# A hybrid decoder layer on one core: the first projection block starts on unscaled k tiles, which are rescaled later

## The chip, the core and the metric

The kernel runs on one core of one Trainium2 chip. The core has a matrix engine (PE, with its weight loads PEld), a vector engine (DVE), an activation engine (ACT), a general engine (POOL) and a queue engine (SP) that issues most of the loads. Each engine works through its own list of instructions in order and waits on semaphores of the others. The metric is the time of one execution in microseconds (us).

## The reference, cut to what matters

One decoder layer: RMSNorm of x (512 tokens by 2048), one wide input projection, two token mixers (an mLSTM and a gated DeltaNet branch), an output projection, merge gates, a residual and a final RMSNorm, all in float32. What matters here is the front:

```python
y = x * rsqrt(mean(x * x, -1) + 1e-6) * norm_w      # u, 512 x 2048
proj = u @ w_in                                      # 2048 x 20528
```

Each token of u carries a factor, rsqrt(...), that is known only when the whole row of x has been read and squared; norm_w is a factor per channel. A product with unscaled channels can be scaled by the token's factor afterwards, since that factor is common to all channels of the token.

## The kernel before

x is cut into 4 chunks of 128 tokens, the 2048 channels into 16 k tiles of 128 (`KT`). A float32 product is made of three passes in the type fp32r: high half by high half, low by high, high by low. So every operand is split: ACT casts a copy to the high half (`split_hi`, L140) and DVE subtracts to get the low half (`split_lo`, L143). u is kept with tokens on the free side, as `uh` (high) and `ul` (low), 16 tiles of 128 x 512.

**Start.** SP loads the four chunks of x, two halves each. ACT and DVE square and sum each chunk, POOL takes the power -1/2 (L304), ACT and DVE scale the chunk (`scale_x`, L290 and L292). Only then can PE transpose the four 128 x 128 pieces of a k tile (`make_u`, L313); ACT writes `uh`, DVE `ul` (L314, L315), both with norm_w's column as scale.

**The four front blocks** (`proj_cm`, L257 to L259) are 256 columns each of q and k. A block goes over 8 pairs of k tiles; the weights of one pair are one *part* here: a load into `wr`, a cast into `wh` and a difference into `wl`, in rotating sets of 4 buffers (`NSPL`), prepared up to 3 parts ahead. Parts 0 to 7 are block 1, 8 to 15 block 2, 16 to 23 block 3, 24 to 31 block 4. A part has 24 products in two half steps (one for each 128 columns), and after each half step `tick()` lets small jobs run. In block 1 the same loop also makes the u tiles, two ahead, and the products of the 48 gate columns (`gate_products`, L324, L325), eight k tiles late.

**Jobs beside blocks 2 to 4.** `gates()` turns the gate columns into per-token rows: transposes of the block's sum `gr0` on PE (`pgt`, L401), some 30 short DVE operations that compute softplus, and 20 ticks later twelve transposes (`pri`, `prf`, `prg`, L443 to L445) of their results, the scans, and a last set of transposes (`pc`). `u_sums()` adds tiles of u for the stage that follows (L373 to L384). `lead()` loads that stage's first weights. The seven stage (PE lines L578 to L580) begins when block 4 ends.

**What sets the order.** PE's list is as written. On the other engines a list scheduler sets it by priority and a timeline of its own.

Of the kernel before, what the change touches and what calls it, by code (L numbers as in the profile page):

```python
# [15 lines left out]
P = 128  # L16
# [12 lines left out]
GLAG = 8  # L29
# [29 lines left out]
def hybrid_body(  # L59
# [91 lines left out]
    plan = [("i", (ML_Q, ML_K)[a] + b * NB, k) for a, b in QK for k in range(0, KT, KP)]  # L151
# [10 lines left out]
    limit = [nfront]  # L162

# [11 lines left out]
    def split_next():  # L175
        raw, nk, n = raws[len(parts)]
        with tc.high_priority(offset=2 * PRIO if len(parts) > SAHEAD else 0):
            hi = wp.tile([P, nk, n], F32R, tag="wh", name="wh", bufs=NSPL)
            lo = wp.tile([P, nk, n], F32R, tag="wl", name="wl", bufs=NSPL)
            with ExitStack() as first:  # L180
                if not parts:
                    first.enter_context(behind("V"))
                    first.enter_context(behind("A"))
                elif len(parts) == 1:
                    first.enter_context(tc.issue_after(done["V"]))
                    first.enter_context(tc.issue_after(done["A"]))
                split_hi(hi, raw)
                split_lo(lo, raw, hi)
        parts.append((hi, lo))

    def prepare(i):
        while len(raws) < min(limit[0], i + RAHEAD + 1):
            load_raw()
        while len(parts) < min(limit[0], i + SAHEAD + 1):
            split_next()
# [50 lines left out]
    def proj_cm(col0, before=None):  # L246
        ps = [psj.tile([P, S], F32, tag="pj", name="pj") for _ in range(2)]
        for kt0 in range(0, KT, KP):
            hi, lo = next_w("i", col0, kt0)
            if before is not None:  # L250
                for k in range(KP):
                    before(kt0 + k)
            for j in range(2):
                for k in range(KP):
                    kt = kt0 + k
                    wsl = slice(j * P, (j + 1) * P)
                    T.matmul(ps[j], hi[:, k, wsl], uh[:, kt, :], start=(kt == 0), stop=False)  # L257
                    T.matmul(ps[j], hi[:, k, wsl], ul[:, kt, :], start=False, stop=False)  # L258
                    T.matmul(ps[j], lo[:, k, wsl], uh[:, kt, :], start=False, stop=(kt == KT - 1))  # L259
                tick()  # L260
        return ps
# [4 lines left out]
    xts = []  # L266
    for c in range(NC):
        xt = p0.tile([P, D], F32, tag=f"x{c}", name=f"xt{c}")
        for i in range(2):
            nc.sync.dma_start(xt[:, i * HD:(i + 1) * HD], x[c * P:(c + 1) * P, i * HD:(i + 1) * HD])  # L270
        xts.append(xt)
    for _ in range(2):
        load_raw()
# [3 lines left out]
    wgh, wgl = wgp[:, :, 0:48], wgp[:, :, 64:112]  # L277
    G.memset(wgp[:, :, 48:64].bitcast(F32), 0.0)
    taps = []
    ss = p0.tile([P, NC, 2], F32, tag="ss", name="ss")  # L280
    rs = p0.tile([P, NC], F32, tag="rs", name="rs")
    mhalf = cp.tile([P, NC], F32, tag="mhalf", name="mhalf")
    G.memset(mhalf, -0.5)
    half = cp.tile([P, 2, NC], F32, tag="half", name="half")
    G.memset(half, 0.5)
    sq, done = {}, {}

    def scale_x(c):
        with tc.issue_after(sq["V"]):
            newest["V"] = V.tensor_scalar(out=xts[c][:, 0:HD], in0=xts[c][:, 0:HD], scalar1=rs[:, c:c + 1], scalar2=None,  # L290
                                        op0=ALU.mult).ins
        newest["A"] = A.mul(xts[c][:, HD:D], xts[c][:, HD:D], rs[:, c:c + 1]).ins  # L292

    for c in range(NC):
        xt = xts[c]
        jk = p0.tile([P, HD], F32, tag="jk", name="jk", bufs=2)
        A.activation(jk, xt[:, 0:HD], AF.Square, accum_out=ss[:, c, 0:1])
        jv = p0.tile([P, HD], F32, tag="jv", name="jv", bufs=2)
        sq["V"] = V.scalar_tensor_tensor(out=jv, in0=xt[:, HD:D], scalar=1.0, in1=xt[:, HD:D], op0=ALU.mult, op1=ALU.mult,
                                         accum_out=ss[:, c, 1:2]).ins  # L300
        V.tensor_tensor(out=rs[:, c:c + 1], in0=ss[:, c, 0:1], in1=ss[:, c, 1:2], op=ALU.add)
        V.tensor_scalar(out=rs[:, c:c + 1], in0=rs[:, c:c + 1], scalar1=1.0 / D, scalar2=EPS,
                        op0=ALU.mult, op1=ALU.add)
        G.tensor_tensor(out=rs[:, c:c + 1], in0=rs[:, c:c + 1], in1=mhalf[:, c:c + 1], op=ALU.pow)  # L304
        if c:
            scale_x(c - 1)
    scale_x(NC - 1)

    def make_u(kt):
        pool, tg = ((psw, "wk"), (pso, "o"))[kt % 2]  # L310
        pt = pool.tile([P, S], F32, tag=tg, name="put")
        for c in range(NC):
            T.transpose(pt[:, c * P:(c + 1) * P], xts[c][:, kt * P:(kt + 1) * P], ident)  # L313
        done["A"] = A.activation(uh[:, kt, :], pt, AF.Copy, scale=normc[:, kt:kt + 1]).ins  # L314
        done["V"] = V.scalar_tensor_tensor(out=ul[:, kt, :], in0=pt, scalar=normc[:, kt:kt + 1],  # L315
                                           in1=uh[:, kt, :].bitcast(F32), op0=ALU.mult, op1=ALU.subtract).ins

    UA = 2
    for kt in range(UA):
        make_u(kt)  # L320
    pgr = psw.tile([P, S], F32, tag="wk", name="pgr")

    def gate_products(kt):
        T.matmul(pgr[0:112, :], wgp[:, kt, :], uh[:, kt, :], start=(kt == 0), stop=False, skip_group_check=True)  # L324
        T.matmul(pgr[0:48, :], wgh[:, kt, :], ul[:, kt, :], start=False, stop=(kt == KT - 1), skip_group_check=True)  # L325

    def first_block(kt):
        if kt == 1:
            nc.sync.dma_start(wg[:, :, 0:16], w_in[:, ML_I:ML_I + 16].rearrange("(k p) n -> p k n", p=P))
            nc.sync.dma_start(wg[:, :, 16:48], w_in[:, DN_B:DN_B + 32].rearrange("(k p) n -> p k n", p=P))  # L330
        if kt == 3:
            taps.extend(load_params(p0))
        if kt == 6:
            with tc.issue_after(done["A"]):
                split_hi(wgh, wg)
            with tc.issue_after(done["V"]):
                split_lo(wgl, wg, wgh)
        if kt == 12:
            turn_taps(*taps, psw)
        if kt + UA < KT:  # L340
            make_u(kt + UA)
        if kt >= GLAG:
            gate_products(kt - GLAG)

# [7 lines left out]
    ps = proj_cm(ML_Q, before=first_block)  # L352
    for kt in range(KT - GLAG, KT):
        gate_products(kt)
    gr0 = wp.tile([112, S], F32, tag="tg", name="gr0", bufs=3)
    A.copy(gr0, pgr[0:112, :])
    spill(ps, 0, float(P) ** -0.5)
# [429 lines left out]
    start(gates())  # L787
    start(u_sums(), 7)
    start(lead(), 38)
    for a, b in QK[1:]:  # L790
        spill(proj_cm((ML_Q, ML_K)[a] + b * NB), 2 * QKFIRST * a + 2 * b, 1.0 if a else float(P) ** -0.5, (a, b) == QK[-1])
# [977 lines left out]
```

## Time and profile before

| what | value |
|---|---|
| time, median of 3 runs | 2154.34 us (2153.77 to 2154.91) |
| time of the profiled execution | 2153.98 us |
| its span, first to last instruction | 2152.2 us |
| PE busy | 2122.7 us, 99% |
| DVE busy | 1710.5 us, 79% |
| ACT busy | 1041.6 us, 48% |

The span is what the profile shows; some 1.8 us of the profiled execution's time lie around it. Shares are means over the whole span: the first 20 us, in which x is loaded and scaled, are no part of what the mean tells.

### The profile page before, as it was taken

Reading aid. Unit: us, or ns where it says so; the run is one execution under the profiler, and the core shown is the slowest. Engines: PE = TensorE matmul, PEld = TensorE weight load, DVE = VectorE, ACT = ScalarE, POOL = GpSimd, SP = SyncE. Lnnn points to the kernel's source line nnn. Section 1 sums busy time; section 2 is a strip of 40 time slices with the busy share of each in tenths; the row PEclk is TensorE's granted clock in tenths of the full one; section 3 lists DMA queues with packets and bytes.
Section 4 is the critical chain, followed back from the end, with each engine's and each line's share of the span. In section 5 each row is a group of like instructions: output and inputs, shape, how many; then the busy total and the mean of one; then the engine's idle time right before and its main releaser. Section 6 shows DMA issues by size and latency. Waiting matters only on the chain.

```text
span 2152.2 us, 31876 instructions
## 1 busy us (share of the span) xinstructions
PE 2122.7 (99%) x10544; PEld 1760.0 (82%) x10544; DVE 1710.5 (79%) x2973; ACT 1041.6 (48%) x1994; POOL 431.5 (20%) x651
## 2 busy tenths in 40 slices
PE   6999999999999999999999999999999999999998
PEld 5888888888888888888888888888888888887886
DVE  5888888788888778777757887887887878569887
ACT  5444444445444444444445545556455464345345
POOL 0000000000004000000002335234233263233221
PEclk9999999999999999999999999999999999999999
DMA  5456676667678767776767777767786677778895
GB/s 162 117 193 191 211 215 196 220 202 227 203 228 243 243 195 223 237 231 195 254 201 176 186 178 185 166 181 188 178 222 171 167 183 209 198 231 278 242 301 230
DMA packets 447143, 444.20 MB, mean 206 GB/s; under 512 B 197121, under 2 KB 303842, under 8 KB 446850
## 3 DMA queue, kind: packets, MB, share of 16 engines
q1 hardware_dynamic: 377618, 337.22, 54.7%
q0 software_dynamic: 24752, 72.90, 10.9%
q10 hardware_dynamic: 44608, 32.06, 4.7%
q8 instruction: 82, 1.34, 0.3%
q14 instruction: 83, 0.68, 0.1%
HBM read 348.66 MB, written 97.58 MB: 207 GB/s over the span
## 4 chain that ended last, share of the span: by engine, by line
PE 94%; DMA 2%; DVE 2%; SPq 1%; issue 1%; ACT 0%; ACTq 0%; DVEq 0%; POOLq 0%; POOL 0%
PE ps L579 17%; PE ps L578 17%; PE ps L580 17%; PE pj L257 9%; PE pj L259 9%; PE pj L258 9%; PE py L1391 2%; PE py L1393 2%; PE py L1392 2%; PE pk L909 1%; PE pqk L979 1%; PE pnum L1197 1%; PE pw L1071 1%; PE po L1086 1%; DMA wr<-in_w_in_dram 0%
## 5 line engine op out<-in xcount | busy, mean ns | idle before, releaser
L140 ACT CAST wh<-wr 128x512 fp32r<-128x512 f32 (+1 forms) x522 | 373.7, 717 | 442.3 <-PE pj L258 233.7
L143 DVE TENSOR_TENSOR wl<-wr,wh 128x512 fp32r<-128x512 f32 (+1 forms) x522 | 439.2, 842 | 171.5 <-ACT wh L140 167.6
L257 PE MATMUL pj<-uh,wh 128*128 128x512 f32 x896 | 376.4, 420 | 0.0
L259 PE MATMUL pj<-uh,wl 128*128 128x512 f32 x896 | 351.3, 392 | 0.0
L258 PE MATMUL pj<-ul,wh 128*128 128x512 f32 x896 | 350.6, 391 | 0.0
L579 PE MATMUL ps<-wl,uh 128*128 128x512 f32 x752 | 292.6, 389 | 0.0
L578 PE MATMUL ps<-wh,uh 128*128 128x512 f32 x752 | 292.6, 389 | 0.0
L580 PE MATMUL ps<-wh,ul 128*128 128x512 f32 x752 | 292.5, 389 | 0.0
L140 ACT CAST wh<-t 128x1024 fp32r<-128x1024 f32 x120 | 126.3, 1053 | 298.4 <-PE ps L580 189.9
L578 PE MATMUL ps<-wh,suh 128*128 128x512 f32 x624 | 242.9, 389 | 0.1
L579 PE MATMUL ps<-wl,suh 128*128 128x512 f32 x624 | 242.8, 389 | 0.0
L580 PE MATMUL ps<-wh,sul 128*128 128x512 f32 x624 | 242.7, 389 | 0.0
L533 POOL DMA_DIRECT2D t_d<-ts x104 | 56.6, 545 | 922.3 <-DVE ts L520 854.0
L140 ACT CAST wh<-ts 128x512 fp32r<-128x512 f32 x240 | 148.4, 618 | 186.8 <-DVE ts L538 157.6
L143 DVE TENSOR_TENSOR wl<-t,wh 128x1024 fp32r<-128x1024 f32 x120 | 146.9, 1224 | 82.1 <-ACT wh L140 81.6
L259 PEld LDWEIGHTS pj<-uh,wl 128*128 128x128 f32 x896 | 168.4, 188 | 37.3
L257 PEld LDWEIGHTS pj<-uh,wh 128*128 128x128 f32 x896 | 169.3, 189 | 30.1
L258 PEld LDWEIGHTS pj<-ul,wh 128*128 128x128 f32 x896 | 169.5, 189 | 28.3
L143 DVE TENSOR_TENSOR wl<-ts,wh 128x512 fp32r<-128x512 f32 x240 | 164.5, 686 | 32.8 <-ACT wh L140 31.3
L579 PEld LDWEIGHTS ps<-wl,uh 128*128 128x128 f32 x752 | 141.2, 188 | 29.7 <-DVE wl L143 0.4
L578 PEld LDWEIGHTS ps<-wh,uh 128*128 128x128 f32 x752 | 141.1, 188 | 29.4
L580 PEld LDWEIGHTS ps<-wh,ul 128*128 128x128 f32 x752 | 141.1, 188 | 29.1
(334 smaller groups left out, 3763.8 us busy)
## 6 DMA issues: line engine op xcount, KB each, us to landing
wr<-in_w_in_dram SPq DMA_DIRECT2D x744, 256.0 KB, 3.7
wr<-in_w_out_dram SPq DMA_DIRECT2D x138, 256.0 KB, 4.7
t_d<-ts POOLq DMA_DIRECT2D x104, 256.0 KB, 3.7
wr<-t_d SPq DMA_DIRECT2D x104, 256.0 KB, 3.8
xt<-in_x_dram SPq DMA_DIRECT2D x8, 512.0 KB, 7.1
tg_d<-X ACTq DMA_DIRECT2D x16, 256.0 KB, 4.7
tg_d<-to ACTq DMA_DIRECT2D x16, 256.0 KB, 4.4
v<-v_d SPq DMA_DIRECT2D x8, 512.0 KB, 6.1
```

What stands on the lines that cost most here:

```text
L140: newest["A"] = A.copy(hi, src).ins
L143: newest["V"] = V.tensor_tensor(out=lo, in0=src, in1=hi.bitcast(F32), op=ALU.subtract).ins
L257: T.matmul(ps[j], hi[:, k, wsl], uh[:, kt, :], start=(kt == 0), stop=False)
L258: T.matmul(ps[j], hi[:, k, wsl], ul[:, kt, :], start=False, stop=False)
L259: T.matmul(ps[j], lo[:, k, wsl], uh[:, kt, :], start=False, stop=(kt == KT - 1))
L533: queue.dma_start(t2_d[b % 2, i], ts[:, 0, :])
L578: T.matmul(ps[t], ah, hi, start=(g == "A" and i == 0), stop=False, skip_group_check=True)
L579: T.matmul(ps[t], ah, lo, start=False, stop=False, skip_group_check=True)
L580: T.matmul(ps[t], al, hi, start=False, stop=(i == KH - 1), skip_group_check=True)
L1391: T.matmul(ps[c], uh[:, kt, tsl], hi, start=(kt == ks[0]), stop=False)
L1392: T.matmul(ps[c], uh[:, kt, tsl], lo, start=False, stop=False)
L1393: T.matmul(ps[c], ul[:, kt, tsl], hi, start=False, stop=(kt == ks[-1]))
```

## The change

x is loaded by columns (all tokens of 256, 256, 512, 256 and 768 channels), with weight loads in between. The first ten k tiles (`KU`) are transposed without the token's factor and multiplied into PSUM banks of their own (`rawp`, `rawg`), while the squares are taken beside the steps. From step 8 on the factor is known: tiles 10 to 15 are scaled as before and multiplied into new banks. The factors are turned into a row (`turn_row`, four products), which scales the raw sums (DVE) and, pair by pair, the ten raw tiles of u (`rescale`, `rescaled`): two pairs in block 1, the third half in it, the rest behind it. Block 2 takes the pairs 10, 12, 14 first. The order of ACT and DVE in block 1 is written by hand. `gates()` starts four ticks later.

```diff
-GLAG = 8
+KU = 10
+    KS[QK[1]] = list(range(KU, KT, KP)) + list(range(0, KU, KP))
...
+    XC = [0, 256, 512, 1024, 1280, D]
+    for n in range(len(XC) - 1):
+        o = slice(XC[n], XC[n + 1])
+        with behind("S") if n else ExitStack():
+            newest["S"] = nc.sync.dma_start(xt[:, :, o], xv[:, :, o]).ins
+        if n in (0, 1, 3, 4):
+            with behind("S"):
+                load_raw()
...
+    def split_u(kt, pt):
+        hi, lo = uh[:, kt, :], ul[:, kt, :]
+        if kt < 4 or kt >= KU:
+            A.activation(hi, pt, AF.Copy, scale=normc[:, kt:kt + 1])
+            V.scalar_tensor_tensor(out=lo, in0=pt, scalar=normc[:, kt:kt + 1], in1=hi.bitcast(F32), op0=ALU.mult, op1=ALU.subtract)
+        else:
+            f = whole(kt - 4, 1)[:, 0]
+            A.activation(f, pt.rearrange("p (c t) -> p c t", t=P), AF.Copy, scale=normc[:, kt:kt + 1])
+            split_hi(hi.rearrange("p (c t) -> p c t", t=P), f)
+            split_lo(lo.rearrange("p (c t) -> p c t", t=P), f, hi.rearrange("p (c t) -> p c t", t=P))
...
+    def rescale(p):
...
+            V.tensor_tensor(out=f, in0=hi.bitcast(F32), in1=lo.bitcast(F32), op=ALU.add)
+        else:
+            f = uf[p] = whole(KP * p - 4, KP)
+        V.tensor_tensor(out=f, in0=f, in1=rr, op=ALU.mult)
...
+    SPLITS = {1: 1, 3: 2, 5: 3, 7: 4, 9: 5, 11: 6, 12: 7, 13: 8, 14: 9, 15: 10}
+    def hook(n):
+        if n in SPLITS:
+            split_next()
...
+        if n == 7:
+            split_hi(wgh, wg)
+            split_lo(wgl, wg, wgh)
+            square(A, 2, 2)
+            square(V, 2, 3)
+            token_factors()
+        if n == 8:
+            scale_x(KU, KU + 2)
+            gps["diag"] = factor_row()
+        if n in (9, 10):
+            for kt in range(KU // 2 * (n - 9), KU // 2 * (n - 8)):
+                gate_products(kt)
+        if n == 10:
+            turn_row(gps["diag"])
...
+        if n + 2 < KT:
+            split_u(n + 2, turn_x(n + 2))
...
+        if n in (11, 13, 15):
+            rescale((n - 11) // 2)
+        if n in (12, 14):
+            rescaled((n - 12) // 2)
+        if n == 10:
+            V.tensor_tensor(out=gr0, in0=rawg[0:112, :], in1=rrow[0:112, :], op=ALU.mult)
...
+    with tc.manual_schedule(engines={mybir.EngineType.Activation, mybir.EngineType.DVE}):
...
+        gsum = V.tensor_tensor(out=gr0, in0=gr0, in1=gps["p"][0:112, :], op=ALU.add).ins
+    with behind("A"), tc.issue_after(gsum):
+        rescaled(2)
+        rescale(3)
+        rescale(4)
+        rescaled(3)
+        rescaled(4)
...
-    start(gates())
+    start(gates(), 4)
```

**Place one: the first scaled tile.** On PE before, all tiles are transposed after scaling, so the list begins with the transposes of tile 0, one from each chunk of x:

```order
L108 MATMUL pprm_126<-ident_76,nrow_124 128x16
L313 MATMUL put_174<-ident_76,xt0_108 128x128
L313 MATMUL put_174<-ident_76,xt1_111 128x128
L313 MATMUL put_174<-ident_76,xt2_114 128x128
L313 MATMUL put_174<-ident_76,xt3_117 128x128
L313 MATMUL put_181<-ident_76,xt0_108 128x128
```

In the changed kernel PE begins on tile 0 without any factor, and the transposes of tile 10 (`put_342`), the first that need it, stand at the head of step 8, ahead of that step's products:

```order
L444 MATMUL pj_142<-ul_90,wh_268 128x512
L445 MATMUL pj_142<-uh_89,wl_269 128x512
L331 MATMUL put_342<-ident_76,xt_113 128x128 x4
L443 MATMUL pj_141<-uh_89,wh_306 128x512
L444 MATMUL pj_141<-ul_90,wh_306 128x512
L445 MATMUL pj_141<-uh_89,wl_307 128x512
L443 MATMUL pj_141<-uh_89,wh_306 128x512
L444 MATMUL pj_141<-ul_90,wh_306 128x512
```

Ahead of them on DVE, the steps 6 to 8 of the changed kernel: the low halves of raw tiles 8 and 9 (`ul`), the split of part 4 (`wl_307`), of the gate weights (`wgp`), the last squares of x, the factors (`rs`), and the scaling of tiles 10 and 11 (L311):

```order
L143 TENSOR_TENSOR ul_90<-xt_113,uh_89 128x512
L143 TENSOR_TENSOR wl_307<-wr_167,wh_306 128x512
L143 TENSOR_TENSOR wgp_128<-wg_127,wgp_128 128x16x48
L298 SCALAR_TENSOR_TENSOR jk_140,ss_134<-xt_113 128x768
L303 TENSOR_REDUCE rs_135<-ss_134 128x4
L304 TENSOR_SCALAR rs_135<-rs_135 128x4
L143 TENSOR_TENSOR ul_90<-xt_113,uh_89 128x512
L311 TENSOR_SCALAR xt_113<-xt_113,rs_135 128x256 x2
```

What moved: the factors stood ahead of all transposes and now stand behind eight steps of them.

**Place two: the gate numbers on DVE.** Before, the last two of them (L431, L434, in `sml`) stand ahead of the split of part 19 (`wl_743`):

```order
L143 TENSOR_TENSOR wl_713<-wr_692,wh_712 128x512
L429 TENSOR_TENSOR sml_546<-sml_546 128x96
L384 TENSOR_TENSOR sul_95<-X_517,suh_94 128x768
L430 SCALAR_TENSOR_TENSOR sml_546<-sml_546 128x96
L384 TENSOR_TENSOR s4l_516<-X_517,s4h_515 128x256
L431 TENSOR_SCALAR sml_546<-sml_546 128x4x8
L434 SCALAR_TENSOR_TENSOR sml_546<-sml_546 128x4x16
L143 TENSOR_TENSOR wl_743<-wr_710,wh_742 128x512
```

In the changed kernel the corresponding operations L545 to L552 stand behind the split of part 23 (`wl_893`), with u sums (`X`, `sul`, `s4l`) in between:

```order
L143 TENSOR_TENSOR wl_893<-wr_839,wh_892 128x512
L493 TENSOR_TENSOR X_548<-X_548 128x256
L495 TENSOR_TENSOR X_548<-X_548 128x256
L546 TENSOR_SCALAR sml_601<-sml_601 128x96
L494 TENSOR_TENSOR X_548<-X_548 128x256
L545 TENSOR_TENSOR sml_601<-sml_601 128x96
L496 TENSOR_TENSOR X_548<-X_548 128x256
L546 TENSOR_SCALAR sml_601<-sml_601 128x96
```

Four rows further on the last eight of these nineteen rows:

```order
L545 TENSOR_TENSOR sml_601<-sml_601 128x96
L546 TENSOR_SCALAR sml_601<-sml_601 128x96
L545 TENSOR_TENSOR sml_601<-sml_601 128x96
L546 TENSOR_SCALAR sml_601<-sml_601 128x96
L547 TENSOR_TENSOR sml_601<-sml_601 128x96
L548 SCALAR_TENSOR_TENSOR sml_601<-sml_601 128x96
L549 TENSOR_SCALAR sml_601<-sml_601 128x4x8
L552 SCALAR_TENSOR_TENSOR sml_601<-sml_601 128x4x16
```

What moved: part 19's place is taken by part 23. On ACT the casts of parts 19 to 23 (`wh_773`, 796, 818, 841, 892) stand so; the fifth of them takes the buffer that the first has, as there are four:

```order
L140 CAST wh_773<-wr_741 128x512
L473 ACTIVATE qk0_766<-pj_556 128x512
L474 DMA qk_d_73<-qk0_766 128x512
L500 CAST suh_94<-X_548 128x768
L140 CAST wh_796<-wr_771 128x512
L500 CAST s4h_546<-X_548 128x256
L140 CAST wh_818<-wr_794 128x512
L140 CAST wh_841<-wr_816 128x512
L500 CAST suh_94<-X_548 128x768
L500 CAST s4h_546<-X_548 128x256
L140 CAST wh_892<-wr_839 128x512
```

**Place three: PE at the gate transposes.** Before, `pri`, `prf` and `prg` come in the middle of part 18 (`wh_712`):

```order
L257 MATMUL pj_738<-uh_89,wh_712 128x512
L258 MATMUL pj_738<-ul_90,wh_712 128x512
L259 MATMUL pj_738<-uh_89,wl_713 128x512
L443 MATMUL pri_797<-ident_76,sml_546 8x128
L444 MATMUL prf_798<-ident_76,sml_546 8x128
L445 MATMUL prg_799<-ident_76,sml_546 16x128
```

In the changed kernel they come when part 19 (`wh_773`) is through:

```order
L250 MATMUL pj_770<-uh_89,wh_773 128x512
L251 MATMUL pj_770<-ul_90,wh_773 128x512
L252 MATMUL pj_770<-uh_89,wl_774 128x512
L561 MATMUL pri_857<-ident_76,sml_601 8x128
L562 MATMUL prf_858<-ident_76,sml_601 8x128
L563 MATMUL prg_859<-ident_76,sml_601 16x128
```

What moved: three half steps later in the blocks, and behind the last product of the part whose buffer the cast of part 23 takes. The row between, `prf`, reads what L549 writes.

## Rows read from the trace of the kernel before

**Rows 1.** The page: the chain of waits that ended last, by engine.

```profile
PE 94%; DMA 2%; DVE 2%; SPq 1%; issue 1%; ACT 0%; ACTq 0%; DVEq 0%; POOLq 0%; POOL 0%
```

**Rows 2.** Waits of PE in total: line, releaser, us, times, longest.

```profile
PE pprm L108 <- POOL rs L304: 14.5, 1, 14.5
PE put L313 <- DVE xt L290: 2.1, 2, 1.3
...
PE ps L578 <- DVE X L1415: 1.5, 1, 1.5
```

**Rows 3.** The chain in order of time, 0 to 160 us: start, us, what.

```profile
17.95 3.03 PE put L313 x13
...
21.41 0.43 PE pj L258
...
23.54 0.36 PE pj L257
...
25.04 0.87 PE put L313 x8
25.91 0.23 PE pj L257
...
58.72 0.39 PE pgt L401 x4
```

**Rows 4.** Timeline of PE, three points: start, us, operation.

```profile
57.17 0.40 PE L257 MATMUL pj<-uh,wh 128*128 128x512 f32 x1
...
86.20 0.27 PE L443 MATMUL pri<-ident,sml 128*8 128x128 f32 x1
...
125.32 0.39 PE L578 MATMUL ps<-wh,suh 128*128 128x512 f32 x1
```

**Rows 5.** Timeline of ACT, 0 to 62 us: the first work on x, its wait.

```profile
4.62 1.06 ACT L297 ACTIVATE jk<-xt 128x1024 f32<-128x1024 f32 x1 [2.59 <-DMA xt<-in_x_dram]
```

**Rows 6.** Timeline of POOL, 0 to 62 us: the last power.

```profile
16.56 0.55 POOL L304 TENSOR_TENSOR rs<-rs,mhalf 128x1 f32<-128x1 f32 x1 [2.07 <-DVE rs L302]
```

**Rows 7.** Groups of ACT by shape, 0 to 175 us: xcount, busy us, mean ns, idle before.

```profile
L140 ACT CAST wh<-wr 128x512 fp32r<-128x512 f32 x40 | 24.5, 619 | 35.2 <-PE pj L258 31.6 <-DMA wr<-in_w_in_dram 3.0 <-PE pj L259 0.5
L314 ACT ACTIVATE uh<-put,normc 128x512 fp32r<-128x512 f32 x16 | 10.5, 686 | 1.4 <-PE put L313 1.2
...
L297 ACT ACTIVATE jk<-xt 128x1024 f32<-128x1024 f32 x4 | 4.2, 1053 | 5.2 <-DMA xt<-in_x_dram 5.2
...
L140 ACT CAST wgp<-wg 128x768 fp32r<-128x768 f32 x1 | 0.8, 834 | 0.0
```

**Rows 8.** Groups of DVE by shape, 0 to 175 us.

```profile
L143 DVE TENSOR_TENSOR wl<-wr,wh 128x512 fp32r<-128x512 f32 x40 | 27.3, 686 | 16.1 <-ACT wh L140 13.9 <-PE put L313 2.2
L315 DVE SCALAR_TENSOR_TENSOR ul<-put,normc,uh 128x512 fp32r<-128x512 f32 x16 | 11.5, 747 | 0.7 <-ACT uh L314 0.2
...
L373 DVE TENSOR_TENSOR X<-uh,ul 128x1024 f32<-128x1024 f32 x8 | 9.7, 1217 | 0.0
L384 DVE TENSOR_TENSOR sul<-X,suh 128x768 fp32r<-128x768 f32 x8 | 7.6, 953 | 0.5 <-ACT suh L382 0.4
...
L375 DVE TENSOR_TENSOR X<-X 128x256 f32<-128x256 f32 x8 | 3.4, 419 | 0.1
L384 DVE TENSOR_TENSOR s4l<-X,s4h 128x256 fp32r<-128x256 f32 x8 | 3.3, 417 | 0.0
...
L427 DVE TENSOR_TENSOR sml<-sml 128x96 f32<-128x96 f32 x7 | 1.8, 253 | 0.1
L428 DVE TENSOR_SCALAR sml<-sml 128x96 f32<-128x96 f32 x7 | 1.4, 206 | 0.1
```

**Rows 9.** Timeline of DVE, 79 to 81 us: the end of the gate numbers.

```profile
78.12 0.95 DVE L384 TENSOR_TENSOR sul<-X,suh 128x768 fp32r<-128x768 f32 x1
78.99 0.25 DVE L430 SCALAR_TENSOR_TENSOR sml<-sml 128x96 f32<-128x96 f32 x1
...
79.58 0.22 DVE L434 SCALAR_TENSOR_TENSOR sml<-sml 128x64 f32<-128x64 f32 x1
```

More of the change, by code (lines that the diff above doesn't have):

```diff
@@ L162, in hybrid_body @@
     limit = [nfront]
+    ahead = [0]
     def load_raw():
@@ L179, in split_next @@
             lo = wp.tile([P, nk, n], F32R, tag="wl", name="wl", bufs=NSPL)
[L180 to L188, printed above, removed]
+            split_hi(hi, raw)
+            split_lo(lo, raw, hi)
         parts.append((hi, lo))
@@ L193, in prepare @@
             load_raw()
-        while len(parts) < min(limit[0], i + SAHEAD + 1):
+        while len(parts) < min(limit[0], i + ahead[0] + 1):
             split_next()
@@ L283, in hybrid_body @@
-    G.memset(mhalf, -0.5)
+    rrow = p0.tile([P, S], F32, tag="rrow", name="rrow")
     half = cp.tile([P, 2, NC], F32, tag="half", name="half")
     G.memset(half, 0.5)
[L286 to L306, printed above, removed]
@@ new lines, in square, with token_factors @@
+    def square(eng, n, c):
+        w = SQ[n].stop - SQ[n].start
+        xc, to = xt[:, c, SQ[n]], ss[:, c, n:n + 1]
+        if eng is V:
+            V.scalar_tensor_tensor(out=jv[:, 0:w], in0=xc, scalar=1.0, in1=xc, op0=ALU.mult, op1=ALU.mult, accum_out=to)
+        else:
+            A.activation(jk[:, 0:w], xc, AF.Square, accum_out=to)
+    def token_factors():
+        V.reduce_sum(out=rs, in_=ss, axis=mybir.AxisListType.X)
+        V.tensor_scalar(out=rs, in0=rs, scalar1=1.0 / D, scalar2=EPS, op0=ALU.mult, op1=ALU.add)
+        G.tensor_tensor(out=rs, in0=rs, in1=mhalf, op=ALU.pow)
@@ new lines, in scale_x, with factor_row @@
+    def scale_x(a, b):
+        for c in range(NC):
+            xc = xt[:, c, a * P:b * P]
+            if c % 2:
+                V.tensor_scalar(out=xc, in0=xc, scalar1=rs[:, c:c + 1], scalar2=None, op0=ALU.mult)
+            else:
+                A.mul(xc, xc, rs[:, c:c + 1])
+    def factor_row():
+        diag = p0.tile([P, NC, P], F32, tag="diag", name="diag")
+        for c in range(NC):
+            V.tensor_scalar(out=diag[:, c, :], in0=ident, scalar1=rs[:, c:c + 1], scalar2=None, op0=ALU.mult)
+        return diag
@@ L311, in make_u, with turn_row, turn_x @@
+    def turn_row(diag):
+        pr = psw.tile([P, S], F32, tag="wk", name="prow")
+        for c in range(NC):
+            T.matmul(pr[:, c * P:(c + 1) * P], ones, diag[:, c, :], start=True, stop=True)
+        A.copy(rrow, pr)
+    def turn_x(kt):
+        pool, tg = ((psw, "wk"), (pso, "o"))[kt % 2 if kt < KU else 0]
         pt = pool.tile([P, S], F32, tag=tg, name="put")
         for c in range(NC):
-            T.transpose(pt[:, c * P:(c + 1) * P], xts[c][:, kt * P:(kt + 1) * P], ident)
@@ new lines, in hook, with first_block @@
+        if n in (11, 13, 15):
[4 more added lines that the diff above has]
+            V.tensor_tensor(out=gr0, in0=rawg[0:112, :], in1=rrow[0:112, :], op=ALU.mult)
+        if n in (12, 14):
+            V.scalar_tensor_tensor(out=qk0[n // 2 - 6], in0=rawp[n // 2 - 6], scalar=QS, in1=rrow, op0=ALU.mult, op1=ALU.mult)
+    def first_block():
+        ps = rawp
+        for n in range(KT):
+            kt0, j = n - n % KP, n % KP
+            if not j:
+                hi, lo = next_w("i", ML_Q, kt0)
+            hook(n)
+            if n == KU:
+                ps = [pso.tile([P, S], F32, tag="o", name="pj") for _ in range(2)]
+            for k in range(KP):
+                kt = kt0 + k
+                wsl = slice(j * P, (j + 1) * P)
+                T.matmul(ps[j], hi[:, k, wsl], uh[:, kt, :], start=(kt in (0, KU)), stop=False)
+                T.matmul(ps[j], hi[:, k, wsl], ul[:, kt, :], start=False, stop=False)
+                T.matmul(ps[j], lo[:, k, wsl], uh[:, kt, :], start=False, stop=(kt in (KU - 1, KT - 1)))
+            if j and kt0 >= KU:
+                for k in range(KP):
+                    gate_products(kt0 + k)
+            tick()
+        return ps
```

124 lines of the change are left out of this document (74 added, 50 removed).

## The prediction

> **What bounds the kernel now.** I read the chain of waits first: PE holds 94% of it [rows 1]. So I took next what PE waits for. Over the whole span it waits 14.5 us for its first transpose, 2.1 us for scaled chunks of x, and afterwards never longer than 1.5 us at a time [rows 2]. Whatever lets PE begin earlier is therefore gained to the end, and whatever it waits for later is lost to the end, unless the work behind shrinks. The chain in order of time shows the start: from 17.95 PE runs unbroken; 13 transposes take 3.03 us, 0.233 each, the first products 0.43 each, and from about 23.6 on a product takes 0.23 and 8 transposes 0.87, 0.109 each [rows 3]. These are the array's two levels, 1.2 and 2.4 GHz: 5.6 us at the lower one, of which half, 2.8 us, is lost. Three points of PE's timeline are my marks: block 2 begins at 57.17, the gate transposes come at 86.20, the seven stage begins at 125.32 [rows 4]. Behind that last mark the lists of DVE and ACT hold the same operations in the same order in both kernels, and PE's list is as written, so I compare the two kernels there and carry the difference to the end.
>
> **The start: minus 12.9 us.** The first 512 KB of x are worked on at 4.62 [rows 5]. The changed kernel's first piece has as many bytes, is issued one place later (behind norm_w) and lies in runs of 1 KB in place of 4 KB; I take 5.04. Nearest rows bound it: 4.6, if neither matters, and 6.0, if the runs cost a quarter. PE's unbroken stretch so begins 12.9 us earlier (12.0 to 13.3). Into it come three slow transposes that lay ahead of 17.95 before, 0.7 us, the four products of the factor row, for which the nearest row is four transposes, 0.44 us [rows 3], and about 0.6 us of short waits (the second piece of x behind the first two tiles, a low half in step 6).
>
> **Tile 10: plus 4.6 us.** The factors are now made beside the raw steps, and the transposes of tile 10 stand at the head of step 8 and wait for them. PE: 16 slow transposes, 9 slow and 3 fast products from 5.04 put tile 4's transposes at 13.4; six steps of four transposes (0.44) and six products (0.23 each), 1.81 a step, and 0.3 of waiting, end at 24.5. ACT can take up tile 4 at 13.95 and then has no pause. A raw tile costs it an activation (0.686) and a cast that depends on it (0.619) where before it was one activation [rows 7]; operations that don't depend on each other overlap by some 0.08, so 1.26 a tile, six tiles 7.6. Three casts of parts add 1.6, the gate weights 0.75 [rows 7]. Three squares of 768 columns have no row of their own; between 0.62 for 512 columns and 1.05 for 1024 [rows 7], with the sum's readout, I take 0.94 each, 2.8. Together 12.75: ACT is through at 26.7. DVE's last square, which has waited behind the gate weights' low half, ends at 27.2; two tiny operations, POOL's power of 0.55 [rows 6] and the hand-overs put the factors at 28.3, two short scalings on ACT put tile 10 at 29.1. PE has waited 4.6 us. If the array is fast earlier and squares cost what 512 columns do, 3; if x's third piece is late, 6.5.
>
> **The end of block 1: plus 2.4 us.** From tile 12's low half (39.2: ten raw gate products a step, the factor row and its copy lie between) DVE has no pause worth a row. Up to the sum of the gate columns it has five 1024-wide adds and products and two 1024-wide differences of the rescaling, 1.14 each (1.217 less the overlap), 8.0; six part splits at 0.605, 3.6; eight operations of the kind of L315 at 0.66 (four low halves, four on the q columns, which ACT did before), 5.3; two sums of the gate columns and the taps, 1.65 [rows 8]. With 0.9 of waiting for ACT that is 19.4, until 58.6. PE would be there at 56.2. So it loses 2.4: about 1.0 at tile 15, the rest at `pgt`. Bounds: 1 and 4, as the broadcast row and the four-dimensional views of the rescaling have no row of their own; the nearest, L373 [rows 8], is what I used.
>
> **The gate transposes: plus 6.8 us.** This is the wait that decides. Before, the gate numbers were done at 79.8 [rows 9], and PE came for them at 86.20 [rows 4]: 6.4 us to spare. In the changed lists PE comes three half steps later in the blocks, when part 19 is through, and DVE has them behind the split of part 23. That split needs ACT's cast, and the cast needs the buffer of part 19, which PE gives back with the very last product ahead of `pri`. So the order alone makes PE wait for one cast (0.619 [rows 7]), one split (0.686) and nineteen operations: four of 256 columns at 0.42, one of 768 at 0.95, another 256 at 0.42, and thirteen of 96 columns or fewer at 0.2 to 0.25 [rows 8], 6.0 end to end, 5.4 with the overlap of 0.08 that the rows show (0.95 long, the next begins 0.87 later [rows 9]). 5.4 and 1.3 and the hand-overs: 6.8 us, 6.0 to 7.5. And DVE isn't there much earlier: its work from 39.2 to that split is 46.3 us (the 18.5 above, then three 1024-wide rescaled differences and two products, eleven splits, three groups of u sums and a begun fourth, and the first half of the gate operations), so it comes to it at 86 to 87, when part 19 ends at 86.5. Were the buffer free earlier, next to nothing would be gained; where DVE is later, the wait grows by that. PE's `prf` holds up all products behind it.
>
> **The clock behind that wait: plus 2.8 us.** After 1.5 us [rows 2] the products go on at the upper level; after the 14.5 us at the start they begin at the lower one and lose 2.8 [rows 3]. No row lies between, so 0 and 2.8 are the ends. 6.8 us is half of the one and over four times the other; I take 2.8. For the 4.6 us at tile 10, in the middle between both, I take 0 and leave 2.8 to a rival.
>
> **The seven stage.** Its first weights go into buffers that the gate rows hold until the `pc` transposes, which also come three half steps later. From these transposes to the first split of that weight there are about 16 us (load 6, DVE's queue 8, cast and split), the blocks leave 18 with the clock at either level. I cost it at nothing; were that cover gone, at most 2 us.
>
> **Sum.** -12.9 + 0.7 + 0.4 + 0.6 + 4.6 + 2.4 + 6.8 + 2.8 = +5.4 us at the mark of 125.32, and from there to the end. The profiled execution took 2153.98, which is 0.36 below the median of the runs: 2159.4 us. Block 2 would begin at about 51.7 (5.5 earlier than before), the gate transposes at 93, the seven stage at 131.
>
> **Rivals.** (1) The clock stays up. All waits as above, but the array does not fall to the lower level behind the gate transposes: +2.6, 2156.6 us, which is no slower as far as can be told. For it: the level is kept over 1.5 us [rows 2]. Against: PE does nothing at all for 6.8 us. It decides at the wait's length: below the length that the chip tolerates this holds, above it the forecast.
> (2) The clock falls at tile 10 too. PE's work from tile 10 to the factor row, 8.6 us, and DVE's queue behind it, all start from that row, so up to 2.8 us more: 2162.2. The row says as much for as against, the wait is 4.6 us. By the Trainium skill, page "TensorE: Matmul & The Clock Gate", section "HAM oscillation — how this bites in real kernels", a pause between bursts of products that is long enough returns the array to half its clock; by that rule the gate wait would be followed by slow products and the wait at tile 10 might be, so the time would be the forecast's or this one's. The trace's start agrees with it (0.43 us a product after 14.5 us of nothing); no run here shows a pause of this length later.
> (3) The gate wait does not happen: -12.9 + 0.7 + 0.4 + 0.6 + 4.6 + 2.4 = -4.2, 2149.8 us. That needs the gate numbers some 7 us earlier than the lists allow. For it: only that my reading of the buffer's hand-back could be wrong. Against: DVE's sum alone gives almost the same moment.
> (4) The change does not bring the start forward: were the column pieces so slow that tile 4 waited for x beyond 16, the start would gain some 10 us instead of 12.9: 2162.3. For it: runs of a quarter of the length; against: the first piece is all that tiles 0 and 1 need, and the third has until 13 to come.
>
> **How the numbers follow.** Forecast 0.45, rival 1 0.26, rival 2 with 4 0.19, rival 3 0.10. About 0.2%, 4.3 us, is what a measurement of this kernel tells from no change, so slower begins at 2158.6 and faster ends at 2150.0. Of the forecast's own range, 2157 to 2162, two thirds lie above: 0.30; with rival 2, 0.18, and a fifth of rival 1, 0.05, slower is 0.53. Faster is two thirds of rival 3, 0.07. Same is the rest, 0.40. The range leaves out some 0.1 at each end: 2152.0, below rival 1 by what shorter waits at tile 10 and in block 1 would give (1.6 and 1.4) and reaching towards rival 3, and 2164.5, above rival 2 by a later x.
>
> **What would show it.** First transpose at about 5.0; ACT without a pause from 14 to 27; PE idle before the transposes of tile 10 (about 4.6) and, above all, before `prf` (about 6.8, released by a DVE operation of the gate numbers); products of 0.43 behind it; DVE without a pause from 39 to 93; the seven stage at 128 to 131. I am wrong if PE has no wait of several us at `prf`, if ACT has pauses between 14 and 27, or if the stretches behind the seven stage's beginning differ by more than 1 us.

## The result and the profile after

The changed kernel takes 2164.92 us, median of 4 runs (2164.34 to 2165.32), against 2154.61 for the kernel before on the same chip: +10.3 us, ratio 1.0048, 95% interval 1.0035 to 1.0060. It is slower, as forecast, but by twice as much (2159.4 was forecast), and 0.4 us above the range of 2152.0 to 2164.5. The profiled execution took 2165.32, span 2163.2 (before 2153.98 and 2152.2).

These are PE's waits in total after the change (line, releaser, us in all, times, longest). Line numbers are those of the changed kernel; beyond the diff they are 118 higher than before.

```profile
PE prf L562 <- DVE sml L549: 6.3, 1, 6.3
PE put L331 <- ACT xt L313: 5.4, 1, 5.4
PE put L331 <- DMA xt<-in_x_dram: 3.6, 2, 2.1
...
PE ps L696 <- DVE X L1533: 1.5, 1, 1.5
...
PE pgt L519 <- DVE gr L460: 0.8, 1, 0.8
PE put L331 <- DVE ul L345: 0.7, 1, 0.7
```

The 14.5 us at the start [rows 2] is gone. In its place stand 6.3 us at the gate transposes and 5.4 us at tile 10, both foreseen in place and nearly in length, 3.6 us for x itself, of which 1.5 lie behind PE's first transposes, and 2.5 for norm_w in front of them.

PE's timeline after, at the places of [rows 3, 4] (start, us, operation; in brackets the idle time before and its releaser):

```profile
4.81 1.97 PE L331 MATMUL put<-ident,xt 128*128 128x128 f32 x8 [2.07 <-DMA xt<-in_x_dram]
8.27 1.12 PE L331 MATMUL put<-ident,xt 128*128 128x128 f32 x4 [1.49 <-DMA xt<-in_x_dram]
...
14.80 0.60 PE L331 MATMUL put<-ident,xt 128*128 128x128 f32 x4
...
31.73 1.11 PE L331 MATMUL put<-ident,xt 128*128 128x128 f32 x4 [5.37 <-ACT xt L313]
...
34.34 0.63 PE L444 MATMUL pj<-ul,wh 128*128 128x512 f32 x1
34.77 0.44 PE L445 MATMUL pj<-uh,wl 128*128 128x512 f32 x1
35.05 0.40 PE L372 MATMUL pgr<-uh,wgp 128*112 128x512 f32 x1
...
41.51 1.05 PE L324 MATMUL prow<-diag,ones 128*128 128x128 f32 x8
...
56.61 0.39 PE L250 MATMUL pj<-uh,wh 128*128 128x512 f32 x1
...
97.23 0.38 PE L562 MATMUL prf<-ident,sml 128*8 128x128 f32 x1 [6.28 <-DVE sml L549]
...
134.97 0.39 PE L696 MATMUL ps<-wh,suh 128*128 128x512 f32 x1
```

PE's transposes begin at 4.81; before, three came from 14.71 on and the unbroken stretch began at 17.95, 13.1 us later than 4.81. But block 2 begins at 56.61, where it began at 57.17: 12.6 of the 13.1 us are spent again within block 1. The seven stage's first product, the mark used from here on, stands at 134.97 against 125.32 [rows 4], 9.65 later.

The clock in five stretches of the changed kernel (window, PE busy and its instructions, granted clock as a share of 2.4 GHz, DMA share, GB/s):

```profile
24.40:31.70 7.30, 1.96 (x11) 0.98 0.51 144
31.70:34.70 3.00, 2.98 (x9) 0.50 0.00 0
34.70:36.00 1.30, 1.30 (x7) 0.94 0.00 0
97.20:102.90 5.70, 5.67 (x19) 0.50 0.00 0
102.90:105.00 2.10, 2.10 (x10) 0.95 0.00 0
```

Behind both long waits the array worked at 1.2 GHz, 3 us behind tile 10's and 5.7 us behind the gate's. The slow products are those that begin 0.43 apart (0.63 long, pipelined), the fast ones begin 0.23 apart.

### The profile page after: what moved, and what is told of

The parts are those of the page before. It is cut to its first block, busy times and chain, and to the rows that moved or that the text cites. A ratio compares the mean times of both kernels' runs of the same rounds, so it can differ in the third digit from the quotient of the medians.

```text
span 2163.2 us, 31910 instructions
## 1 busy us (share of the span) xinstructions
PE 2129.7 (98%) x10552; PEld 1763.4 (82%) x10552; DVE 1725.5 (80%) x2995; ACT 1045.1 (48%) x2005; POOL 430.1 (20%) x649
## 5 line engine op out<-in xcount | busy, mean ns | idle before, releaser
L250 PE MATMUL pj<-uh,wh 128*128 128x512 f32 x864 | 363.6, 421 | 0.0
L252 PE MATMUL pj<-uh,wl 128*128 128x512 f32 x864 | 338.9, 392 | 0.0
L251 PE MATMUL pj<-ul,wh 128*128 128x512 f32 x864 | 338.4, 392 | 0.0
L697 PE MATMUL ps<-wl,uh 128*128 128x512 f32 x752 | 292.7, 389 | 0.4 <-DVE wl L143 0.4
L697 PE MATMUL ps<-wl,suh 128*128 128x512 f32 x624 | 242.9, 389 | 0.0
L252 PEld LDWEIGHTS pj<-uh,wl 128*128 128x128 f32 x864 | 162.6, 188 | 36.1
L250 PEld LDWEIGHTS pj<-uh,wh 128*128 128x128 f32 x864 | 163.4, 189 | 28.8
L251 PEld LDWEIGHTS pj<-ul,wh 128*128 128x128 f32 x864 | 163.5, 189 | 27.2
L697 PEld LDWEIGHTS ps<-wl,uh 128*128 128x128 f32 x752 | 141.1, 188 | 30.3 <-DVE wl L143 1.0
```

Source lines behind the costliest of these rows:

```text
L250: T.matmul(ps[j], hi[:, k, wsl], uh[:, kt, :], start=(kt == ks[0]), stop=False)
L697: T.matmul(ps[t], ah, lo, start=False, stop=False, skip_group_check=True)
```

## The experiments

Two theories were set against each other. **A**: the loss is two waits on PE's own path and the slow array behind them; take away what makes PE wait and the time comes back. **B**: DVE has too much to do between 44 and 97 us, where it hardly pauses; whatever is taken away in one place comes back as a wait in another. A mark and a wait come from one profiled execution, a time is a median of several. The seven kernels below the first two rows ran on another chip than these; each ratio is to the kernel before on its own chip, there 22 runs with a median of 2154.15 (the first four) or 2153.85 (the next three).

| kernel | mark | wait in front of tile 10 | wait at `prf` | time | ratio to before, 95% |
|---|---|---|---|---|---|
| before | 125.32 | none | none | 2154.61 | 1 |
| changed | 134.97 | 5.37 | 6.28 | 2164.92 | 1.0035 to 1.0060 |
| waits filled | 131.74 | 0.82 | 0.86 | 2161.69 | 1.0019 to 1.0044 |
| products first | 129.13 | 2.09 | 6.29 | 2159.82 | 1.0016 to 1.0034 |
| squares first | 134.28 | 4.20 | 6.29 | 2162.12 | 1.0022 to 1.0046 |
| sums later | 126.63 | 5.38 | 0.28 | 2156.53 | 1.0004 to 1.0021 |
| gates at once | 132.61 | 5.37 | none | 2161.18 | 1.0021 to 1.0045 |
| products first and sums later | 122.98 | 2.09 | 0.28 | 2152.48 | 0.9987 to 1.0004 |
| these and two edits more | 120.60 | 1.06 | 0.28 | 2151.54 | 0.9979 to 0.9997 |

The 2.09 us of two rows stand in front of the gate products, which there come ahead of tile 10; tile 10 itself then follows without a wait.

**1. The waits filled with useless work.**

```diff
+        if n == 8:
+            fill = psw.tile([P, S], F32, tag="wk", name="fill")
+            for i in range(20):
+                T.matmul(fill, uh[:, 0, 0:P], uh[:, 0, :], start=True, stop=True)
         if n + 2 < KT:
             split_u(n + 2, turn_x(n + 2))
...
+        for i in range(24):
+            T.matmul(prg, uh[:, 0, 0:P], uh[:, 0, :], start=True, stop=True)
         for c in range(NC):
```

> The changed kernel with work added and none taken away: 20 products of 512 columns into a spare PSUM bank ahead of tile 10's transposes, and 24 ahead of the gate transposes, where PE waited 5.4 and 6.3 us; 0.227 each, so 4.5 and 5.4 us, which fit into the waits. Theory A (the pauses cost the clock on top of their length): the four transposes and six products behind the first wait took 3.3 us where 1.8 is their time at the upper level, 1.5 lost; behind the second, twelve transposes and nine products lost 2.8. Both go: about 4.3 us less than the changed kernel, 2160.6, and no product of 0.43 behind either wait. Theory B (the slow products have another cause than the idle array, such as what DVE and ACT do at that time): the two stretches stay slow and the time stays at 2164.9 or above.

PE's timeline of this kernel, around tile 10, and at the gate transposes with the products behind them:

```profile
26.94 4.71 PE L419 MATMUL fill<-uh 128*128 128x512 f32 x20
32.47 0.84 PE L331 MATMUL put<-ident,xt 128*128 128x128 f32 x4 [0.82 <-ACT xt L313]
36.84 0.60 PE L331 MATMUL put<-ident,xt 128*128 128x128 f32 x4
...
96.75 0.27 PE L568 MATMUL prf<-ident,sml 128*8 128x128 f32 x1 [0.86 <-DVE sml L553]
...
98.44 0.39 PE L252 MATMUL pj<-uh,wl 128*128 128x512 f32 x1
98.67 0.39 PE L250 MATMUL pj<-uh,wh 128*128 128x512 f32 x1
```

44 more products, and the kernel is 2.8 us nearer to the kernel before (+7.5 against +10.3). From `prf` to the mark it takes 34.99 where the changed kernel took 37.74: 2.75 us is the price of the clock behind the gate wait in this pair of executions, for which I had taken 2.8. It is the highest of four: behind the same wait the stretch took 36.48 in experiment 2, 37.65 in experiment 3 and 36.89 in the repeat of experiment 7, so 1.5, 2.7 and 1.9 us. From tile 10's transposes to tile 11's it takes 4.37, not 5.66: 1.3 us there; behind the same wait the stretch took 6.29 in experiment 4 and 6.41 in experiment 5, so 1.9 and 2.0. Theory A holds for the clock: an idle array is what makes the products behind slow. The mark gained 3.2 and not the sum of 4.0, since x's second piece came 0.7 later in this execution.

**2. The raw gate products ahead of tile 10.**

```diff
-        if n in (9, 10):
-            for kt in range(KU // 2 * (n - 9), KU // 2 * (n - 8)):
+        if n in (8, 9):
+            for kt in range(8) if n == 8 else range(8, KU):
                 gate_products(kt)
```

> The changed kernel, with the raw gate products of tiles 0 to 7 at the head of step 8, before tile 10's transposes, and those of tiles 8 and 9 in step 9 (five tiles each in steps 9 and 10 before). The gate weights are split at 28.2, so 16 products of 0.227 stand between 28.2 and about 31.9, where PE waited for the factors until 31.7. Theory A (tile 10's wait is a loss on PE's own path, and what comes after it starts from the factor row): tile 12's transposes, at 42.4, come about 5 us earlier (3.6 of work moved into the wait, 1.5 of clock), block 2 begins 4 to 5 us earlier, and the whole is at 2160 to 2161. If the 2 us pause before the gate products costs the clock as 5.4 us did: 3.6 us, 2161.3. Theory B (DVE's amount of work sets the end of block 1 and the gate numbers, whatever PE does): the wait grows at tile 15 and at the gate transposes, and less than 2 us is left, 2163 or more.

PE, the first of the sixteen products and tile 10's transposes behind the last:

```profile
28.57 0.45 PE L372 MATMUL pgr<-uh,wgp 128*112 128x512 f32 x1 [2.09 <-DVE wgp L143]
...
32.33 0.60 PE L331 MATMUL put<-ident,xt 128*128 128x128 f32 x4
```

As theory A said: the wait for the factors is covered, and tile 12's transposes come at 37.80 in place of 42.40. The gate transposes are reached 4.6 us earlier, and the wait there did not grow (6.29). Nothing was given back at tile 15 (0.7, as in the changed kernel). The time, 2159.8, is just below the 2160 to 2161 expected. Of the mark's 5.8 us, 4.6 were there at `prf`; 1.3 came behind it, where the slow stretch was shorter in this execution (36.48 from `prf` to the mark, not 37.74).

**3. Squares and factors ahead of the gate weights, raw tiles 8 and 9 in a buffer of their own.**

```diff
+    xf = p0.tile([P, 2, S], F32, tag="xf", name="xf")
     def whole(kt, n):
+        if kt > 3:
+            return xf[:, kt - 4:kt - 4 + n, :].rearrange("p k (c t) -> p k c t", t=P)
...
-            split_hi(wgh, wg)
-            split_lo(wgl, wg, wgh)
             square(A, 2, 2)
             square(V, 2, 3)
             token_factors()
+            split_hi(wgh, wg)
+            split_lo(wgl, wg, wgh)
```

> The changed kernel with the last squares and the factors listed ahead of the gate weights' split on ACT and DVE, and the raw tiles 8 and 9 kept in a buffer of their own, where they were written over columns of x whose squares DVE was still to make (ACT waited 1.2 us there). By the trace of the changed kernel DVE's last square (28.2) then comes at about 26.8, and tile 10's transposes (31.7) at about 30.3. Theory A (tile 10 waits for the squares, which wait for these two things): 1.4 us less at tile 10, PE idle 4.0; the time 2163.5, or 2162 if 4.0 us of idling leave the clock up. Theory B (the sums of x and the power on POOL set the moment): no change, tile 10 at 31.7.

The wait shrank from 5.37 to 4.20, but tile 10's transposes came at 31.34 and not at 30.3: x's second piece was 0.8 later here, and with it all of block 1. The four transposes still took 1.12 us, the slow figure. So the squares' place is worth 1.2 us at tile 10, and not 1.4, since POOL's power took 1.63 us here and 1.33 in the changed kernel; why is not shown. And 4.2 us of idling cost the clock too: 5.44 to tile 11's transposes, 1.1 more than with the waits filled. The mark gained 0.7 and the time more (+8.0 against +10.3), but the two intervals overlap.

**4. The sums of u later.**

```diff
-    start(u_sums(), 7)
+    start(u_sums(), 15)
```

> The changed kernel with the sums of u for the seven stage started 15 half steps into block 2, and not 7. The gate numbers then have two 1024-wide sums and their differences fewer before them on DVE, 7 to 8 us of work, and stand ahead of the part split that needed the last product of PE before the gate transposes. Theory A (the wait at the gate transposes comes from the place of the gate numbers in DVE's list): the 6.3 us of waiting and the 2.8 to 3.1 of clock behind it go; the time is about 9.4 us less, 2155.5, and the seven stage begins at about 125.6. Theory B (DVE has more work than time there, so what is moved behind shows up as waits for parts or for the sums): PE waits elsewhere in blocks 2 to 4 or in the seven stage's first products, and the time is 2160 or more.

PE at the gate transposes and at the mark:

```profile
91.64 0.27 PE L562 MATMUL prf<-ident,sml 128*8 128x128 f32 x1 [0.28 <-DVE sml L549]
...
126.63 0.39 PE L696 MATMUL ps<-wh,suh 128*128 128x512 f32 x1
```

One number, and the wait, the clock behind it and 7.9 us of the loss are gone (+2.4 against +10.3). From `prf` to the mark it takes 34.99, as with the waits filled, so nothing came back in the blocks; behind the mark PE waited 1.2 us for low halves at L697 (0.8 in the changed kernel) and 1.1 at L1510, some 1700 us later (none there), which is all that theory B kept. The place of the gate numbers in DVE's list was the cause. A row of ACT and two of DVE in the changed kernel show how it works:

```profile
90.65 0.62 ACT L140 CAST wh<-wr 128x512 fp32r<-128x512 f32 x1 [1.06 <-PE pj L251]
```
```profile
91.30 0.69 DVE L143 TENSOR_TENSOR wl<-wr,wh 128x512 fp32r<-128x512 f32 x1 [0.31 <-ACT wh L140]
...
97.09 0.22 DVE L552 SCALAR_TENSOR_TENSOR sml<-sml 128x64 f32<-128x64 f32 x1
```

DVE had caught up: it stood still for 0.31 us, waiting for the cast of part 23, which waited for the buffer that PE gave back with the last product that reads it, at L251 (begun at 90.22, the last but one ahead of `pri`). Thirteen of the nineteen operations listed behind that split are gate numbers. That is why the wait was 6.28, 6.29 and 6.29 in three kernels whose PE came there at 90.95, 86.4 and 90.3: the split begins when PE is through, wherever that falls. But DVE was there only 0.3 us earlier, so its work ahead of the split would have made PE wait nearly as long. The edit takes both away, two sums of u and the place behind the split, and no run separates them.

**5. The gates at once, as before the change.**

```diff
-    start(gates(), 4)
+    start(gates())
```

> The changed kernel with the gates started at once behind block 1, as before the change, and not four half steps later. Theory A (the gate numbers' place in the lists sets the wait): their transposes from the gate columns then stand at the head of block 2, at 56.6, and the sum of these columns on DVE is done at 62.8, so PE waits 6.2 there in place of 0.8, with slow products behind it (some 2 us); the gate numbers are listed ahead of nineteen other operations on DVE and are through before PE comes for them, so the 6.3 and 2.8 us at the gate transposes go. Together about 2 us less than the changed kernel, 2163: the later start moves a wait from one place to another. Theory B (the delay of four half steps is what makes PE wait, and nothing takes its place): 9 us less, 2156.

PE, the transposes of the gate columns and two products behind them:

```profile
64.17 0.97 PE L519 MATMUL pgt<-ident,gr 112*128 112x112 f32 x4 [4.84 <-DVE gr L460]
64.82 0.78 PE L250 MATMUL pj<-uh,wh 128*128 128x512 f32 x1
65.39 0.63 PE L251 MATMUL pj<-ul,wh 128*128 128x512 f32 x1
```

The wait moved, as theory A said, to `pgt`, with the slow products behind it, and the one at `prf` went. It was 4.8 and not 6.2, since these transposes come one half step into block 2, not at its head. (A half step is six products here and a part twelve; the 24 given above for a part are wrong.) So the later start of the gates was worth a wait of 4 us at `pgt` and cost one of 6 us at `prf`. This part of the change alone made it 2 to 4 us slower: 2.4 by the marks, 3.5 from tile 12's transposes to the mark (89.05 in place of 92.57), as block 1 ended 1.2 later in this execution, and 3.0 by the times (+7.3 without it, +10.3 with it), whose intervals overlap.

**6. Edits 2 and 4 together, and once more with two others.** The second kernel also splits the gate weights in step 6 in place of step 7 (the four lines of experiment 3 moved to `n == 6`) and has the buffer `xf` of experiment 3.

> The changed kernel with both edits: the raw gate products of tiles 0 to 7 ahead of tile 10's transposes, and the sums of u started 15 half steps into block 2. Alone they brought the seven stage's first product 5.8 and 8.3 us forward, from 134.97. Theory A (the two losses are independent, each on PE's own path): 120.8 for that mark, 4.5 us earlier than before the change, and 2150.5 to 2152 for the whole, faster than the kernel before. Theory B (DVE's work is the bound behind block 1, so the gains overlap): the mark at 124 or later, and no faster than the kernel before.

> The kernel with both edits, and two more: the gate weights split a step earlier, so that PE's raw gate products follow the products of step 7 without the pause of 2.1 us, and raw tiles 8 and 9 in a buffer of their own, so that ACT doesn't wait 1.2 us for squares of x. Theory A (the pause in front of the gate products is still on PE's path): about 1 us less than with both edits alone, block 2 beginning 1 us earlier; the squares come 0.9 later for the gate weights' split and 1.2 earlier for the buffer, so tile 10 waits 0 to 1. Theory B (the factors, not the gate weights, set tile 10's time): block 2 begins at the same time as with both edits, and the time is the same.

Together the two edits bring the mark to 122.98, between the two theories and 12.0 us ahead of the changed kernel where their sum would be 14.2; the time is that of the kernel before, as far as can be told. Of the missing 2.2, the 1.3 that experiment 2 had gained behind `prf` could not be gained twice, and 1.6 are the clock: sixteen products took 5.3 us where experiment 2 needed 3.8 for them (the two overshoot by 0.6, about what the executions differ by). Here eight of the sixteen began 0.43 apart behind the pause:

```profile
28.34 0.46 PE L372 MATMUL pgr<-uh,wgp 128*112 128x512 f32 x1 [2.09 <-DVE wgp L143]
28.64 0.39 PE L373 MATMUL pgr<-ul,wgp 128*48 128x512 f32 x1
28.87 0.51 PE L372 MATMUL pgr<-uh,wgp 128*112 128x512 f32 x1
29.18 0.63 PE L373 MATMUL pgr<-ul,wgp 128*48 128x512 f32 x1
29.61 0.63 PE L372 MATMUL pgr<-uh,wgp 128*112 128x512 f32 x1
...
33.66 0.60 PE L331 MATMUL put<-ident,xt 128*128 128x128 f32 x4
```

Without that pause, in the second kernel, the products run on from step 7 at full speed and tile 10 waits only 1.1 us:

```profile
29.58 0.40 PE L376 MATMUL pgr<-ul,wgp 128*48 128x512 f32 x1
31.04 0.84 PE L331 MATMUL put<-ident,xt 128*128 128x128 f32 x4 [1.06 <-ACT xt L313]
```

Its mark is 120.60, 4.7 us ahead of the kernel before, and at 2151.54 us it is faster than both kernels: ratio 0.9988, interval 0.9979 to 0.9997. That is 0.1%, at the edge of what a measurement tells. The gain over the first of the two was 2.4 us by the marks, more than the 1 us expected, as the pause had cost the clock as well; by the times it was 0.9, and the intervals overlap. What each of the two added edits gives was not tried.

**7. Does the same pause always cost the clock?** Experiment 2 kept 2.4 GHz behind its pause of 2.09 us, the kernel with both edits did not, and their code is the same up to there. Both were run once more, unchanged, on the chip of the changed kernel.

> The same kernel as the one with the raw gate products ahead of tile 10, once more. There PE paused 2.09 us before these products and they then ran at 0.23 each; in the kernel with both edits, which is the same up to there, the pause was 2.09 too and eight of the products ran at 0.43. Theory A (after a pause of this length the level differs from execution to execution): this look may show either, and one of the two repeated kernels shows another level than before. Theory B (the kernel decides it): products of 0.23 here again, and of 0.43 in the repeat of the other.

> The same kernel as the one with both edits, once more. Theory A (the level after a pause of 2.1 us differs from execution to execution): products of 0.23 or 0.43 after the pause, not bound to what they were before (0.43). Theory B (the kernel decides it): 0.43 again, for some 3 us.

PE in the repeat of experiment 2:

```profile
28.97 0.45 PE L372 MATMUL pgr<-uh,wgp 128*112 128x512 f32 x1 [2.08 <-DVE wgp L143]
...
30.19 0.46 PE L373 MATMUL pgr<-ul,wgp 128*48 128x512 f32 x1
30.45 0.63 PE L372 MATMUL pgr<-uh,wgp 128*112 128x512 f32 x1
30.88 0.63 PE L373 MATMUL pgr<-ul,wgp 128*48 128x512 f32 x1
...
34.31 0.38 PE L331 MATMUL put<-ident,xt 128*128 128x128 f32 x2
```

(The view ends inside the four transposes of the last line.) Now this kernel fell to the lower level too, some 1.5 us after the pause, the sixteen products took 5.3 us, and its mark was 131.50 and not 129.13. The repeat of the other fell again (mark 122.98 both times). So it differs from execution to execution: of four, one kept the level. The chip alone does not decide it, since the execution that kept the level and one that fell ran on the same; what does is not shown. The repeats also showed how much the rest of the kernel moves by itself: from the mark to the end of the span, where their code is the same, it took 2027.2 us in one and 2029.3 in the other, and 2026.7 in the first execution with both edits.

## Why the prediction was wrong

The mechanism was right: the start is gained, and two waits that the change makes, at tile 10 and at the gate transposes, take more than that back. The size was wrong, and most of it in one step. By stages, in us:

| step of the prediction | forecast | measured | from |
|---|---|---|---|
| the start | -12.9 | -13.1 | 4.81 against 17.95 |
| from the first transposes to tile 4's | 8.4 | 10.0 | 4.81 to 14.80 |
| from tile 4's to tile 10's | 15.7 | 16.9 | 14.80 to 31.73 |
| the clock behind tile 10 | 0 | 1.3 to 1.5 | experiment 1; 3.32 in place of 1.80 up to 35.05; 1.9 and 2.0 in two other executions |
| block 2 begins | 51.7 | 56.61 | |
| the wait at `pgt` | 1.4 | 0.8 | waits of PE |
| the wait at `prf` | 6.8 | 6.3 | waits of PE |
| the clock behind `prf` | 2.8 | 2.75 | experiment 1; 1.5 to 2.7 in three other executions |
| the mark | +5.4 | +9.65 | 134.97 against 125.32 |
| from the mark to the end | 0 | +1.35 | spans less marks |

- **Tile 10: the step that failed.** The prediction said "two short scalings on ACT put tile 10 at 29.1"; it came at 31.7. For the clock behind that wait it took 0, and 1.3 to 1.5 was measured. In the terms of its sum, the wait of 4.6 measured 5.4, the clock's 0 was 1.3 to 1.5, and the 0.6 of short waits was 1.8 (1.49 for x's second piece, 0.31 for a low half). Block 2 began 4.9 us later than forecast, more than the whole miss at the mark (4.25).
- Three things made tile 10 late. First, ACT took up tile 4 at 15.77, where the prediction had 13.95. x's second piece was late, which put tile 3 back, and ACT then stood 1.63 us, since raw tile 4 is written over columns of x that DVE was still squaring. In all ten executions of the changed kernel and its variants ACT began on tile 4 2.93 to 2.94 us after it began on tile 3, whether PE had started tile 4's transposes at 13.78 or at 14.85; so it was not tile 4 itself that it waited for. Second, "ACT ... then has no pause" was wrong once more: for raw tile 8 it stood 1.18 us in the same way. I had counted the operands that an operation reads and not who still reads what it overwrites. Third, POOL's power, which I took from a row of 128x1 [rows 6], has four columns here and takes 1.33, not 0.55. Together that is 3.8 us; tile 10 was 2.6 late, so the rest of the way was 1.2 shorter than I had it. Rows of ACT, DVE and POOL in the changed kernel:

```profile
12.84 0.69 ACT L344 ACTIVATE uh<-put,normc 128x512 fp32r<-128x512 f32 x1 [1.61 <-PE put L331]
...
15.77 0.69 ACT L348 ACTIVATE xt<-put,normc 128x512 f32<-128x512 f32 x1 [1.63 <-DVE jk L298]
...
24.71 0.69 ACT L348 ACTIVATE xt<-put,normc 128x512 f32<-128x512 f32 x1 [1.18 <-DVE jk L298]
```
```profile
28.21 0.95 DVE L298 SCALAR_TENSOR_TENSOR jk<-xt 128x768 f32<-128x768 f32 x1
```
```profile
29.80 1.33 POOL L305 TENSOR_TENSOR rs<-rs,mhalf 128x4 f32<-128x4 f32 x1 [28.01 <-DVE rs L304]
```

- The rest of block 1 held within 1 us; about half of it is the factor row: four products of plain f32 show as eight instructions and 1.05 us, 0.9 until the next begins, where I had 0.44 from four transposes.
- **The gate transposes: right**, in length and in cause (experiment 4). That "the order alone makes PE wait" is what the 0.31 us of idle DVE show; that a buffer freed earlier would gain next to nothing fits them, but was not tried. The clock there was right in cause (experiment 1); its size of 2.8 was partly luck, as it was taken from the start, behind a pause of 14.5 us, and three other executions of this wait paid 1.5 to 2.7.
- The weight given to rival 2 was too small. It said 2162.2, with the clock falling at both waits, and that is what happened, though tile 10's fall cost about half of its 2.8 us; it had 0.19 together with another. The rest of the way to 2164.9 is mostly tile 10's lateness, which stands in no rival. Rival 1 fell with experiment 1, rival 3 with the wait itself, rival 4 with the start, which was gained; only the second piece of x was late (PE waited 1.5 us for it), and not the third. By the Trainium skill, page "TensorE: Matmul & The Clock Gate", section "HAM oscillation — how this bites in real kernels", a long enough pause between bursts costs half the clock; here that held for pauses of 4.2, 4.8, 5.4 and 6.3 us, and for 2.1 us in three executions of four.
- Of the prediction's own signs of being wrong two came in: ACT had pauses, and the stretches behind the mark differ by 1.35 us. These 1.35 are not shown to belong to the change: two kernels with the same code there differ by 2.1 us on the same chip (experiment 7).

## What to carry to other kernels

Work taken out of a start is worth its length only if nothing in the stage behind it makes PE stand still; price each new wait with the slow products behind it (here 1.3 to 2.0 us on top of 5.4, and 1.5 to 2.75 on top of 6.3), and fill it with products whose operands are already there, as the gate products did for tile 10. When a buffer is reused in place, look for who still reads it, as well as for who made what is written. And a chain of small operations listed behind a split that needs PE's own last product can't be ready when PE comes for it, however idle its engine is: move it ahead of that split, here by starting later what stands in front of it.

## What had not been expected of the hardware

The same code with the same pause of 2.1 us kept 2.4 GHz in one execution and fell to 1.2 GHz in three, each time at a price of 1.6 us, and the fall came 0.5 to 1.5 us after the products had begun again. POOL's power took 0.55 us for 128x1 and, but for one execution, 1.33 for 128x4; there (experiment 3) it took 1.63. The profile's granted clock does not show the slow stretch of the start: it reads 1.00 from 18.00 to 23.50 before the change, where products began 0.43 apart, and 0.50 behind the later waits, where they did so too.
